# Where the split activations lie, and when each step of a pair's preparation is issued, in a hybrid attention and SwiGLU block

## The chip, the cores and the metric

The kernel runs on one core of a Trainium2 chip. The metric is device time in microseconds (us) of one execution; lower is better. TensorE (PE in the profile) multiplies; VectorE (DVE), ScalarE (ACT) and GpSimd (POOL) prepare operands; SyncE (SP) issues most loads, POOL the accumulating ones. Every engine works its own queue in order, and engines wait for each other by semaphores.

## The reference, cut to what matters

```python
xn = rms_norm(x, norm1_g)                    # x: 256 tokens x 2048
proj = xn @ w_in                             # 2048 x 5120: q, k, v, conv columns
att, u = diff_attention(...), conv_branch(...)
h = x + concat([att, u]) @ w_out             # 2048 x 2048
hn = rms_norm(h, norm2_g)
a, bu = hn @ w_gate, hn @ w_up               # 2048 x 5632 each
y = h + (silu(a) * bu) @ w_down              # 5632 x 2048
```

All of it is float32. The five weight matrices, about 200 MB, are read once.

## The kernel before, in words

**Split products.** A float32 product is made of three fast ones. Each operand is split in `hi` (rounded to the format fp32r) and `lo` (the rest, rounded too), and PE adds hi x hi, lo x hi and hi x lo in one PSUM bank. The activations are the stationary operand (128x128), loaded once per matmul; the weights are the moving one (128x512). The split activations of the input projection, of `w_out` in part, of the normalized `h` and later of the gated rows lie in two long tiles `lhi` and `llo`, the `arena`. Other activations lie in tiles of their own (`chi`/`clo`, `ahi`/`alo`, `fhi`/`flo`, `mchi`, `mahi`).

**Chunks.** All weights are cut in chunks, and `run_chunks` walks through them: at chunk t it issues what chunks ahead of t need, and then the matmuls of t. A plain chunk or "two" (`multiply_two`, 12 matmuls) holds two 128x512 weight tiles: loaded to `raw` (four buffers), cast by ACT to `whi` (L328), subtracted by DVE to `wlo` (L337). For a chunk marked `by_dma`, ACT writes -raw to `wlo` (L331) and a POOL DMA adds the weights a second time (L332), so that DVE has nothing to do.

**Pairs.** From the second gate/up block on, half of the contraction goes by a scheme of seven products in place of eight (`multiply_pair`, 21 matmuls): two contraction tiles times two sets of 512 columns make four weight tiles (`wb`, 1 MB, two buffers). Their preparation has these steps: the load; `wt`, four sum forms of the tiles, by DVE (L964 to L966, one buffer); `wh`, the casts of seven forms by ACT (L967, L968; two buffers); and the lo parts by DVE: `wla` (L978, L979; two buffers) and `wlb` (L988, L989; one buffer). `wlb` is the last reader of `wb`, so the load of the next pair but one waits for it, and all loads behind it in SP's queue wait too. The list `PRODUCTS` gives the order of the seven: PSUM bank, activation form, weight form.

**Blocks.** A gate/up block (512 columns of gate and of up; ten of them by this scheme, j = 1 to 10) has four pairs `s` and eight twos `g`, `u`; upper case marks `by_dma`. A down block has four pairs and eight twos (in the last group three and six); there are six, two behind each group of gate/up blocks (j to 3, j to 7, j to 10). `ORDER`, `FIRST` and `DOWN` give the order of the chunks. After the last pair, `bank_sums` drains its PSUM banks: ACT copies bank Q1 (L1104), DVE adds the other five into SBUF tiles (L1106 to L1112); in a gate/up block ACT then applies silu (L1118). The next block's first pair needs these banks. After the last two, `block_done` adds the last two banks, and `transposed` turns the block's result into stationary operands for the down product, at L860: by plain hi/lo (L865, L867) or, for the positions in `pairs` of `DOWN`, as seven forms (`pair_forms`, L877 to L892). This work is spread over the next block by generators that go on at each `resume()`.

**Leads.** For chunks of the scheme, loads are issued 5 chunks ahead, `by_dma` rounds 5, other rounds 3 (`round_pair`: the sums, then both casts), `wla` and `wlo` 2, `wlb` 1. `round_pair` also issues the `wlb` of the pair before it, if that is still to come.

Of the kernel before, what the change touches and what calls it, by code (L numbers as in the profile page):

```python
# [30 lines left out]
KD = D // P  # L31
N = 512
# [20 lines left out]
XPARTS = (range(0, 2), range(2, 4), range(4, 8), range(8, 12), range(12, 16))  # L53
# [3 lines left out]
AHEAD = 2  # L57
# [27 lines left out]
DOWN = (dict(pairs=((0, 0), (0, 1), (1, 0), (1, 1)), order="sgGsgGsUusUu"),  # L85
        dict(pairs=((4, 0), (4, 1), (5, 0), (5, 1)), order="sgGsgGsUusUu"),
        dict(pairs=((8, 0), (8, 1), (9, 0)), order="sgGsGsUuU"))

LOAD_AHEAD, DMA_AHEAD, HI_AHEAD, LO_AHEAD, REST_AHEAD = 5, 5, 3, 2, 1

TO_TRANSPOSE = 5

# [12 lines left out]
def tile_block(  # L105
# [179 lines left out]
    chunks = []  # L285
# [106 lines left out]
        if c["done"]:  # L392
            start(c["done"](ps))

    def run_chunks():
        n = len(chunks)
        loaded = split = rest = 0
        rounded = [0, 0]

        def load(i):  # L400
            if i in before:
                before[i]()
            chunks[i]["load"](chunks[i])

        def do_round(which, until):
            while rounded[which] < min(n, until):
                c = chunks[rounded[which]]
                if c["by_dma"] == bool(which):
                    c["round"](c)
                rounded[which] += 1  # L410

        for t in range(n):
            load_lead, dma_lead, hi_lead, lo_lead = lead(t)
            while split < min(rounded[0], t + 1 + lo_lead):
                chunks[split]["split"](chunks[split])
                split += 1
            while loaded < min(n, t + 1 + load_lead):
                load(loaded)
                loaded += 1
                if load_lead == lo_lead:  # L420
                    do_round(1, loaded)
                    do_round(0, loaded)
                    chunks[split]["split"](chunks[split])
                    split += 1
            do_round(1, t + 1 + dma_lead)
            do_round(0, t + 1 + hi_lead)
            while split < min(n, t + 1 + lo_lead):
                chunks[split]["split"](chunks[split])
                split += 1
            while rest < min(n, t + 1 + REST_AHEAD):  # L430
                split_rest(chunks[rest])
                rest += 1
# [379 lines left out]
    ffn = {}  # L812
# [23 lines left out]
    def place(g):  # L836

        pairs = DOWN[g]["pairs"]
        at = 7 * len(pairs)
# [111 lines left out]
        src = weights([(w, k, col, N) for w, col in c["sides"] for k in c["ks"]])  # L951
        sp.dma_start(out=c["b"].rearrange("p k n -> p (k n)"), in_=src)

    def round_pair(c):

        fp = ffn["pool"]
        assert "hi" in forms
        if newest:
            split_rest(newest.pop())
        newest.append(c)  # L960
        b = c["b"]
        c["t"] = t = fp.tile([P, 4, N], F32, tag="wt", name="wt")
        c["hi"] = fp.tile([P, 7, N], F32R, tag="wh", name="wh", bufs=2)
        dve.tensor_tensor(t[:, 2:4], b[:, 1:3], b[:, 0:1].to_broadcast([P, 2, N]), ALU.subtract)  # L964
        dve.tensor_tensor(t[:, 1], b[:, 1], t[:, 3], ALU.add)  # L965
        dve.tensor_tensor(t[:, 0], t[:, 1], b[:, 3], ALU.subtract)  # L966
        act.copy(c["hi"][:, 4:], b[:, 1:])  # L967
        act.copy(c["hi"][:, :4], t)  # L968

    newest = []  # L970

    def split_pair(c):

        if "lo" in c:
            return
        b, t, hi = c["b"], c["t"], c["hi"].bitcast(F32)
        lo = ffn["pool"].tile([P, 4, N], F32R, tag="wla", name="wla", bufs=2)
        dve.tensor_tensor(lo[:, 0], b[:, 2], hi[:, 5], ALU.subtract)  # L978
        dve.tensor_tensor(lo[:, 1:], t[:, 1:], hi[:, 1:4], ALU.subtract)  # L979
        c["lo"] = {5: lo[:, 0], 1: lo[:, 1], 2: lo[:, 2], 3: lo[:, 3]}  # L980

    def split_rest(c):
        if "sides" not in c or 0 in c.get("lo", ()):
            return
        split_pair(c)
        b, t, hi = c["b"], c["t"], c["hi"].bitcast(F32)
        lo = ffn["pool"].tile([P, 3, N], F32R, tag="wlb", name="wlb")
        dve.tensor_tensor(lo[:, 1], t[:, 0], hi[:, 0], ALU.subtract)  # L988
        dve.tensor_tensor(lo[:, ::2], b[:, 1::2], hi[:, 4::2], ALU.subtract)  # L989
        c["lo"].update({4: lo[:, 0], 0: lo[:, 1], 6: lo[:, 2]})  # L990

    def sum_bank(c, i):
        sums = c["sums"]
# [5 lines left out]
    def multiply_pair(c):  # L999
        while not c["ready"](c):  # L1000
            resume()
        (fhi, flo), p = c["forms"](), c["p"]
        for n, (q, f, w) in enumerate(PRODUCTS):
            ps = sum_bank(c, q)
            first, last = c["first"].get(q), c["last"].get(q)
            pe.matmul(ps, fhi[:, f, p, :], c["hi"][:, w], start=bool(first), stop=False)  # L1006
# [45 lines left out]
    def fast_block(order, side_u, side_g, pairs, twos, **kw):  # L1052
# [3 lines left out]
        for unit in order:  # L1056
# [43 lines left out]
    def bank_sums(q):  # L1100

        fp = ffn["pool"]
        w1, u2, u3, w4 = (fp.tile([P, N], F32, tag=f"sum{i}", name=f"sum{i}") for i in range(4))
        act.copy(w1, q[Q1])  # L1104
        yield
        dve.tensor_tensor(u2, q[Q6], w1, ALU.add)  # L1106
        dve.tensor_tensor(u3, q[Q7], u2, ALU.add)
        yield
        dve.tensor_tensor(w4, q[Q5], u3, ALU.add)
        dve.tensor_tensor(u2, q[Q5], u2, ALU.add)  # L1110
        dve.tensor_tensor(w1, q[Q2], w1, ALU.add)
        dve.tensor_tensor(u3, q[Q4], u3, ALU.add)  # L1112
        halfway.update(g=(w1, u3), u=(u2, w4))

    def products_done(q):
        yield from bank_sums(q)
        for t in halfway["g"]:
            act.activation(t, t, AF.Silu)  # L1118

    def block_done(j, q):  # L1120
        while "g" not in halfway:
# [9 lines left out]
    def add_to_out(m, n, t):  # L1131
        pool.dma_start(out=out[m * P : (m + 1) * P, n * N : (n + 1) * N], in_=t, accum_op=ALU.add)

    def down_products(n, q, last):
        so_far = None
        if last:
            so_far = ffn["pool"].tile([P, 4, N], F32, tag="wt", name="so_far")[:, :NM]
            pool.dma_start(out=so_far, in_=out[:, n * N : (n + 1) * N].rearrange("(m p) n -> p m n", p=P))
        yield from bank_sums(q)
        for m in range(NM):  # L1140
            add_to_out(m, n + 1, halfway["g"][m])
        if last:
            yield
# [46 lines left out]
    for g, nb in enumerate(FGROUPS):  # L1190
        for j in range(j0, j0 + nb):
            if j:
                gate_up_block(j, FIRST if j == 1 else ORDER)
                continue
# [3 lines left out]
        for n in range(0, D // N, 2):  # L1198
            down_block(g, n)
        j0 += nb  # L1200

    lead = lambda t: ((1,) * 4 if t < len(XPARTS) else (LOAD_AHEAD, DMA_AHEAD, HI_AHEAD, LO_AHEAD)
                      if "kind" in chunks[t] else (AHEAD,) * 4)
# [39 lines left out]
```

## Time and profile before

| | |
|---|---|
| median of 3 runs (lowest to highest) | 1159.44 us (1158.42 to 1162.35) |
| profiled execution: its time, its span | 1157.78 us, 1156.0 us |
| mean granted TensorE clock | 0.973 |
| busy: PE, DVE, ACT, POOL | 1080.6, 912.5, 674.0, 132.9 us |
| bytes by DMA | 247.58 MB, mean 214 GB/s |

The profile is one execution. A group row gives busy time and mean duration of an instruction, then the engine's idle time before it and what ended it. In the windows view each row is a stretch of time with the busy time of every engine in it, the granted clock (1.00 is full speed) and the DMA engines' share. In the timeline each row has the start, the length and, in brackets, the idle time before it.

### The profile page before, as it was taken

To read this page: it belongs to the slowest core of one execution; us is meant where nothing else is said; L and a number is where in the kernel's file an instruction comes from. 1 tells how busy PE (TensorE), PEld (TensorE's weight loads), DVE (VectorE), ACT (ScalarE), POOL (GpSimd) and SP (SyncE) were. 2 spreads that over 40 slices of the span, in tenths; PEclk is the share of its full clock that TensorE was granted. 3 is DMA by queue.
4 is the path that set the end of the run, shared out by engine and by line. 5 is a ranking of instruction groups with operands and counts; after the bars stand their busy time and mean duration, and the time that the engine had idled before them with its cause. 6 is when DMAs were issued, how large, how long until landed. Compare 5 with 4: busy or idle time off the path is not lost. (4 is left out here: it accounts for less than half of the span.)

```text
span 1156.0 us, 13323 instructions
## 1 busy us (share of the span) xinstructions
PE 1080.6 (93%) x4768; PEld 869.8 (75%) x4768; DVE 912.5 (79%) x1252; ACT 674.0 (58%) x857; POOL 132.9 (11%) x180
## 2 busy tenths in 40 slices
PE   8999999999999978999899998897999998999598
PEld 7888888887888856777688776676877776777486
DVE  4799889898665877887886868788788786887865
ACT  7544657656665554766556547466565454755552
POOL 1110112211001000101020201001001020101021
PEclk9999999999999989999899999999999999999899
DMA  8555544445466557779678986776968897778767
GB/s 294 193 191 189 182 164 152 170 153 180 148 203 206 203 173 245 195 248 274 199 242 250 235 274 200 254 200 206 287 205 247 246 249 244 217 247 253 212 154 182
DMA packets 62447, 247.58 MB, mean 214 GB/s; under 512 B 6964, under 2 KB 8430, under 8 KB 54444
## 3 DMA queue, kind: packets, MB, share of 16 engines
q1 hardware_dynamic: 48000, 200.56, 48.0%
q0 software_dynamic: 14320, 46.14, 21.3%
q8 instruction: 37, 0.61, 0.2%
q14 instruction: 30, 0.25, 0.1%
q10 hardware_dynamic: 60, 0.03, 0.0%
HBM read 238.31 MB, written 8.39 MB: 213 GB/s over the span
## 5 line engine op out<-in xcount | busy, mean ns | idle before, releaser
L328 ACT CAST whi<-raw 128x1024 fp32r<-128x1024 f32 (+1 forms) x253 | 260.2, 1045 | 167.8 <-DMA raw<-in_wts_dram 125.6
L337 DVE TENSOR_TENSOR wlo<-raw,whi 128x1024 fp32r<-128x1024 f32 (+1 forms) x181 | 219.0, 1217 | 57.0 <-ACT whi L328 56.6
L968 ACT CAST wh<-wt 128x2048 fp32r<-128x2048 f32 x62 | 118.3, 1908 | 101.9 <-DVE wt L966 101.9
L367 PE MATMUL acc<-whi,lhi 128*128 128x512 f32 (+1 forms) x448 | 170.8, 386 | 3.3 <-ACT lhi L234 2.6
L368 PE MATMUL acc<-whi,llo 128*128 128x512 f32 (+1 forms) x448 | 169.1, 382 | 0.5 <-DVE llo L235 0.4
L979 DVE TENSOR_TENSOR wla<-wt,wh 128x1536 fp32r<-128x1536 f32 x62 | 108.9, 1757 | 64.3 <-ACT wh L968 64.3
L1006 PE MATMUL q<-wh,fhi 128*128 128x512 f32 x280 | 118.1, 422 | 31.8 <-DVE sum L1110 18.0
L332 POOL DMA_DIRECT2D wlo<-in_wts_dram x72 | 67.6, 939 | 634.2 <-ACT wlo L331 500.1
L1024 PE MATMUL q<-whi,chi 128*128 128x512 f32 x320 | 124.8, 390 | 0.0
L1025 PE MATMUL q<-whi,clo 128*128 128x512 f32 x320 | 124.6, 389 | 0.0
L373 PE MATMUL acc<-wlo,lhi 128*128 128x512 f32 (+1 forms) x448 | 116.4, 384 | 0.0
L1007 PE MATMUL q<-wh,flo 128*128 128x512 f32 x280 | 114.5, 409 | 0.0
L524 DVE SCALAR_TENSOR_TENSOR y<-upad,cw,y 128x256 f32<-128x256 f32 x240 | 103.7, 482 | 4.6 <-ACT y L517 4.1
L367 PEld LDWEIGHTS acc<-whi,lhi 128*128 128x128 f32 x448 | 85.3, 190 | 20.7 <-ACT lhi L234 2.8
L368 PEld LDWEIGHTS acc<-whi,llo 128*128 128x128 f32 x448 | 85.4, 191 | 17.7 <-DVE llo L235 0.9
L1006 PEld LDWEIGHTS q<-wh,fhi 128*128 128x128 f32 x280 | 56.0, 200 | 50.1 <-DVE sum L1110 21.4
L373 PEld LDWEIGHTS acc<-wlo,lhi 128*128 128x128 f32 x448 | 79.9, 189 | 16.9 <-DVE wlo L337 0.2
L967 ACT CAST wh<-wb 128x1536 fp32r<-128x1536 f32 x62 | 90.8, 1465 | 2.9 <-PE q L1007 1.5
L1029 PE MATMUL q<-wlo,chi 128*128 128x512 f32 x320 | 86.5, 392 | 0.0
L964 DVE TENSOR_TENSOR wt<-wb 128x1024 f32<-128x1024 f32 x62 | 75.5, 1218 | 3.8 <-DMA wb<-in_wts_dram 3.8
L331 ACT ACTIVATE wlo<-raw 128x1024 fp32r<-128x1024 f32 x72 | 76.0, 1055 | 0.0
L989 DVE TENSOR_TENSOR wlb<-wb,wh 128x1024 fp32r<-128x1024 f32 x62 | 75.5, 1218 | 0.0
(219 smaller groups left out, 1870.9 us busy)
## 6 DMA issues: line engine op xcount, KB each, us to landing
raw<-in_wts_dram SPq DMA_DIRECT2D x251, 512.0 KB, 5.5
wb<-in_wts_dram SPq DMA_DIRECT2D x62, 1024.0 KB, 5.3
wlo<-in_wts_dram POOLq DMA_DIRECT2D x72, 512.0 KB, 8.0
out_dram<-sum POOLq DMA_DIRECT2D x22, 256.0 KB, 8.8
out_dram<-h POOLq DMA_DIRECT2D x8, 256.0 KB, 5.2
h<-in_x_dram SPq DMA_DIRECT2D x6, 256.0 KB, 7.8
h<-in_x_dram SPq DMA_DIRECT2D x4, 128.0 KB, 2.9
raw<-in_wts_dram SPq DMA_DIRECT2D x2, 256.0 KB, 3.9
```

What stands on the lines that cost most here:

```text
L328: act.copy(c["hi"], c["raw"])
L337: dve.tensor_tensor(c["lo"], c["raw"], c["hi"].bitcast(F32), ALU.subtract)
L367: pe.matmul(ps[m], xhi[:, ms], hi[:, j, :], start=c["first"] and j == 0, stop=False)
L368: pe.matmul(ps[m], xlo[:, ms], hi[:, j, :], start=False, stop=False)
L373: pe.matmul(ps[m], xhi[:, ms], lo[:, j, :], start=False, stop=c["last"] and j == nk - 1)
L524: dve.scalar_tensor_tensor(y[:, ct, :], src, wk, y[:, ct, :], ALU.mult, ALU.add)
L968: act.copy(c["hi"][:, :4], t)
L979: dve.tensor_tensor(lo[:, 1:], t[:, 1:], hi[:, 1:4], ALU.subtract)
L1006: pe.matmul(ps, fhi[:, f, p, :], c["hi"][:, w], start=bool(first), stop=False)
L1007: pe.matmul(ps, flo[:, f, p, :], c["hi"][:, w], start=False, stop=False)
L1024: pe.matmul(ps, plain[i][0][:, ms], hi[:, i, :], start=i == 0 and bool(c["first"].get(qs[m])), stop=False)
L1025: pe.matmul(ps, plain[i][1][:, ms], hi[:, i, :], start=False, stop=False)
```

## The change

1. The arena is allocated right after `ident`, ahead of small tiles. Its two tiles start at byte 128 of a 512-byte line of each partition, as nearly all other tiles do; before, at byte 480. Sizes are unchanged.
2. `round_pair` is parted: `pair_sums` (the DVE sums) gets a lead of its own, 4 chunks; the casts stay at 3, `wla` at 2, `wlb` at 1. Loads are issued last in a step, not first.
3. `wla` is now the four sum forms in one instruction of 2048 elements, `wlb` the three raw forms in one of 1536 (before: 512 + 1536, and 512 + 1024).
4. `PRODUCTS` starts with the three sum forms; bank Q1, which was first, is fourth. So `wlb` is first needed by the 12th of a pair's 21 matmuls.
5. `ORDER` and the down orders have the pairs at chunks 0, 2, 5, 7 of 12 and four twos at the end (before: 0, 3, 6, 9 and two). `FIRST` has them at 3, 5, 7, 9 (before 4, 6, 8, 10). Down blocks have three `by_dma` chunks (the last two blocks too) where they had four; `FIRST` four where it had three.
6. `bank_sums` is issued in one piece, not over three `resume()`s. In the first group the down pairs come from j = 1 and 2, not 0 and 1.

```diff
-ORDER = "sgGsgGsUUsUu"
+ORDER = "sGsGgsGsUuUu"
-FIRST = "gugusgsUsGsU"
+FIRST = "gugsGsGsusUU"
-PRODUCTS = ((Q1, 0, 5), (Q6, 5, 1), (Q7, 6, 2), (Q5, 4, 3), (Q2, 1, 6), (Q4, 2, 0), (Q3, 3, 4))
-DOWN = (dict(pairs=((0, 0), (0, 1), (1, 0), (1, 1)), order="sgGsgGsUusUu"),
+PRODUCTS = ((Q6, 5, 1), (Q7, 6, 2), (Q5, 4, 3), (Q1, 0, 5), (Q2, 1, 6), (Q4, 2, 0), (Q3, 3, 4))
+DOWN = (dict(pairs=((1, 0), (1, 1), (2, 0), (2, 1)), order="sGsGgsGsuuuu"),
...
-        dict(pairs=((8, 0), (8, 1), (9, 0)), order="sgGsGsUuU"))
-LOAD_AHEAD, DMA_AHEAD, HI_AHEAD, LO_AHEAD, REST_AHEAD = 5, 5, 3, 2, 1
+        dict(pairs=((8, 0), (8, 1), (9, 0)), order="sGsGgsUuu"))
+LOAD_AHEAD, DMA_AHEAD, SUMS_AHEAD, HI_AHEAD, PART_AHEAD, REST_AHEAD = 5, 5, 4, 3, 2, 1
...
     make_identity(nc, ident)
+    arena = [const.tile([P, 2 * KD, P], F32R, tag=f"l{x}", name=f"l{x}") for x in ("hi", "lo")]
...
-    arena = [const.tile([P, 2 * KD, P], F32R, tag=f"l{x}", name=f"l{x}") for x in ("hi", "lo")]
...
         for t in range(n):
...
+            if "kind" in chunks[t]:
+                until("part", part_of, t + 1 + PART_AHEAD)
+                until("dma", round_of, t + 1 + DMA_AHEAD, lambda c: c["by_dma"])
+                until("sums", sums_of, t + 1 + SUMS_AHEAD)
+                until("round", round_of, t + 1 + HI_AHEAD)
+                until("rest", rest_of, t + 1 + REST_AHEAD)
+                load_until(t + 1 + LOAD_AHEAD)
+            else:
+                until("rest", rest_of, t + 1 + (1 if t < len(XPARTS) else AHEAD))
+            rest_of(t)
             chunks[t]["multiply"](chunks[t])
...
-    def round_pair(c):
+    def pair_sums(c):
...
         if newest:
-            split_rest(newest.pop())
+            part_of(newest.pop())
...
-        act.copy(c["hi"][:, 4:], b[:, 1:])
-        act.copy(c["hi"][:, :4], t)
...
+    def round_pair(c):
+        c["hi"] = ffn["pool"].tile([P, 7, N], F32R, tag="wh", name="wh", bufs=2)
+        act.copy(c["hi"][:, 4:], c["b"][:, 1:])
+        act.copy(c["hi"][:, :4], c["t"])
+
     def split_pair(c):
...
+        c["lo"] = ffn["pool"].tile([P, 4, N], F32R, tag="wla", name="wla", bufs=2)
+        dve.tensor_tensor(c["lo"], c["t"], c["hi"][:, :4].bitcast(F32), ALU.subtract)
 
     def split_rest(c):
...
+        c["lob"] = ffn["pool"].tile([P, 3, N], F32R, tag="wlb", name="wlb")
+        dve.tensor_tensor(c["lob"], c["b"][:, 1:], c["hi"][:, 4:].bitcast(F32), ALU.subtract)
...
-            pe.matmul(ps, fhi[:, f, p, :], c["lo"][w], start=False, stop=bool(last))
+            pe.matmul(ps, fhi[:, f, p, :], c["lo"][:, w] if w < 4 else c["lob"][:, w - 4], start=False, stop=bool(last))
...
         act.copy(w1, q[Q1])
-        yield
         dve.tensor_tensor(u2, q[Q6], w1, ALU.add)
         dve.tensor_tensor(u3, q[Q7], u2, ALU.add)
-        yield
...
```

VectorE's queue where block j = 5 ends and j = 6 begins, before (`wb`, `wt`, `wh`, `wla`, `wlb` as above; `sum` are the drained banks, `q` the banks):

```order
L966 TENSOR_TENSOR wt<-wt,wb 128x512
L978 TENSOR_TENSOR wla<-wb,wh 128x512
L979 TENSOR_TENSOR wla<-wt,wh 128x1536
L1106 TENSOR_TENSOR sum_6210<-q_5913,sum_6209 128x512
L1107 TENSOR_TENSOR sum_6211<-q_5917,sum_6210 128x512
L337 TENSOR_TENSOR wlo<-raw,whi 128x1024
L988 TENSOR_TENSOR wlb<-wt,wh 128x512
L989 TENSOR_TENSOR wlb<-wb,wh 128x2x512
L1109 TENSOR_TENSOR sum_6212<-q_5921,sum_6211 128x512
L1110 TENSOR_TENSOR sum_6210<-q_5921,sum_6210 128x512
L1111 TENSOR_TENSOR sum_6209<-q_5925,sum_6209 128x512
L1112 TENSOR_TENSOR sum_6211<-q_5929,sum_6211 128x512
```

and now:

```order
L1115 TENSOR_TENSOR sum_6117<-q_5864,sum_6116 128x512
L1116 TENSOR_TENSOR sum_6115<-q_5864,sum_6115 128x512
L1117 TENSOR_TENSOR sum_6114<-q_5872,sum_6114 128x512
L1118 TENSOR_TENSOR sum_6116<-q_5876,sum_6116 128x512
L337 TENSOR_TENSOR wlo<-raw,whi 128x1024
L994 TENSOR_TENSOR wla<-wt,wh 128x2048
L981 TENSOR_TENSOR wt<-wb 128x1024
L982 TENSOR_TENSOR wt<-wb,wt 128x512
L983 TENSOR_TENSOR wt<-wt,wb 128x512
L998 TENSOR_TENSOR wlb<-wb,wh 128x1536
L1132 TENSOR_TENSOR sum_6115<-q_5880,sum_6115 128x512
```

Before, the first pair's `wt` and `wla` stand ahead of the bank sums, and its `wlb` between them. Now the sums come first in one piece (the last four are shown), then the first pair's `wla`, the `wt` of the second pair, and the first pair's `wlb` behind that.

ScalarE's queue at the same place, before:

```order
L967 CAST wh<-wb 128x1536
L968 CAST wh<-wt 128x2048
L328 CAST whi<-raw 128x1024
L1104 COPY sum_6209<-q_5909 128x512
L1118 ACTIVATE sum_6209<-sum_6209 128x512
L1118 ACTIVATE sum_6211<-sum_6211 128x512
L328 CAST whi<-raw 128x1024
L331 ACTIVATE wlo<-raw 128x1024
```

and now:

```order
L1112 COPY sum_6114<-q_5868 128x512
L1124 ACTIVATE sum_6114<-sum_6114 128x512
L1124 ACTIVATE sum_6116<-sum_6116 128x512
L989 CAST wh<-wb 128x1536
L990 CAST wh<-wt 128x2048
L328 CAST whi<-raw 128x1024
L331 ACTIVATE wlo<-raw 128x1024
L989 CAST wh<-wb 128x1536
L990 CAST wh<-wt 128x2048
```

Before, both casts of the next block's first pair stand ahead of the copy of bank Q1 and of the silu. Now they come behind the silu, which waits for the bank sums; behind them is a `by_dma` two and then the casts of the second pair.

More of the change, by code (lines that the diff above doesn't have):

```diff
@@ L393, in multiply, with load_until @@
             start(c["done"](ps))
[L395 to L400, printed above, removed]
+    loaded, rounded, parted, whole = [0], set(), set(), set()
+    def load_until(n):
+        while loaded[0] < min(n, len(chunks)):
+            i = loaded[0]
+            loaded[0] += 1
             if i in before:
@@ L403, in load, with sums_of @@
             chunks[i]["load"](chunks[i])
[L405 to L410, printed above, removed]
-        for t in range(n):
[L413 to L432, printed above, removed]
+    def sums_of(i):
+        c = chunks[i]
+        if "sides" in c and "t" not in c:
+            load_until(i + 1)
+            pair_sums(c)
@@ new lines, in round_of, with part_of, rest_of, run_chunks @@
+    def round_of(i):
+        if i not in rounded:
+            rounded.add(i)
+            load_until(i + 1)
+            sums_of(i)
+            chunks[i]["round"](chunks[i])
+    def part_of(i):
+        if i not in parted:
+            parted.add(i)
+            round_of(i)
+            chunks[i]["split"](chunks[i])
+    def rest_of(i):
+        if i not in whole:
+            whole.add(i)
+            part_of(i)
+            if "sides" in chunks[i]:
+                split_rest(chunks[i])
+    def run_chunks():
+        n = len(chunks)
+        at = dict(part=0, dma=0, sums=0, round=0, rest=0)
+        def until(what, do, stop, only=lambda c: True):
+            while at[what] < min(n, stop):
+                if only(chunks[at[what]]):
+                    do(at[what])
+                at[what] += 1
+        for t in range(n):
+            if "kind" in chunks[t]:
[8 more added lines that the diff above has]
+            rest_of(t)
@@ L952, in load_pair @@
         sp.dma_start(out=c["b"].rearrange("p k n -> p (k n)"), in_=src)
[L954 to L956 removed]
+    def pair_sums(c):
         assert "hi" in forms
         if newest:
[L959 to L960 removed]
+            part_of(newest.pop())
+        newest.append(next(i for i, o in enumerate(chunks) if o is c))
         b = c["b"]
[L962 to L963 removed]
+        c["t"] = t = ffn["pool"].tile([P, 4, N], F32, tag="wt", name="wt")
         dve.tensor_tensor(t[:, 2:4], b[:, 1:3], b[:, 0:1].to_broadcast([P, 2, N]), ALU.subtract)
```

26 lines of the change are left out of this document (5 added, 21 removed).

## The prediction

> **What bounds the kernel now.** First the windows view by stage, then the waits, then rows of single steps.
>
> ```profile
> core 0: us, PE busy (x) PEld busy (x) DVE busy (x) ACT busy (x) POOL busy (x), PEclk, DMA share, GB/s
> 0.00:401.88 401.88, 396.12 (x1890) 326.45 (x1891) 320.67 (x526) 240.34 (x449) 50.19 (x85) 1.00 0.53 186
> 401.88:455.48 53.60, 44.53 (x190) 35.99 (x188) 40.32 (x53) 31.38 (x31) 3.55 (x4) 0.90 0.69 226
> 455.48:1072.94 617.46, 572.37 (x2412) 454.80 (x2412) 492.69 (x602) 366.23 (x346) 67.01 (x77) 0.97 0.80 235
> 1072.94:1152.20 79.26, 67.53 (x278) 52.53 (x278) 58.04 (x72) 36.05 (x33) 12.14 (x14) 0.94 0.71 187
> ```
>
> Up to 401.88 (projections, attention, `w_out`, the plain block) PE is the bound. Then run the pair blocks: the first (to 455.48), thirteen more, and the last two down blocks (from 1072.94). There PE idles 9.1 + 45.1 + 11.7 = 65.9 us, and a stretch at half clock loses half its length, so the clock's shortfall costs 10%, 3% and 6% of the three stretches: 5.4 + 18.5 + 4.8 = 28.7 us.
>
> ```profile
> PE q L1006 <- DVE sum L1110: 22.4, 11, 3.1
> DVE wla L979 <- ACT wh L968: 64.3, 50, 1.4
> SPq L952 <- DVE wlb L989: 625.3, 60, 16.2
> 509.19 0.50 PE L1006 MATMUL q<-wh,fhi 128*128 128x512 f32 x1 [2.18 <-DVE sum L1110]
> ...
> 510.97 0.63 PE L1006 MATMUL q<-wh,fhi 128*128 128x512 f32 x1
> 643.86:691.79 47.93, 43.70 (x182) 34.66 (x180) 35.86 (x41) 26.14 (x22) 7.91 (x9) 0.96 0.91 260
> 739.89:789.16 49.27, 45.07 (x188) 35.20 (x189) 40.15 (x56) 30.74 (x32) 4.33 (x5) 0.97 0.75 221
> 789.16:840.82 51.66, 45.57 (x190) 36.40 (x189) 43.13 (x52) 28.26 (x26) 4.33 (x5) 0.93 0.75 219
> ```
>
> A block's first pair waits for the bank sums; a pair's preparation goes DVE, ACT, DVE, and DVE waits for ACT in the middle; every pair load waits for a `wlb`. Behind a gap of 2.18 us, matmuls take 0.63 us in place of 0.39: half clock. The last three rows are gate/up blocks (j = 4, 6, 7).
>
> **The arena.** Three starts on, with `lhi`/`llo` and then with `chi`/`clo`; medians in the source view; weight loads:
>
> ```profile
> 382.88 0.40 PE L368 MATMUL acc<-whi,llo 128*128 128x512 f32 x1
> ...
> 383.59 0.40 PE L367 MATMUL acc<-whi,lhi 128*128 128x512 f32 x1
> ...
> 402.81 0.39 PE L1024 MATMUL q<-whi,chi 128*128 128x512 f32 x1
> ...
> 403.49 0.39 PE L1025 MATMUL q<-whi,clo 128*128 128x512 f32 x1
> ...
> L367 PE MATMUL acc<-whi,lhi 128*128 128x512 f32 x384 | 153.7, 400 | 0.0
> L373 PE MATMUL acc<-wlo,lhi x448: 277/394/585, 8.3 to 401.6; 128*128 128x512 f32 x128, 128*128 128x256 f32 x22
> L1029 PE MATMUL q<-wlo,chi x320: 388/389/481, 403.7 to 1071.4; 128*128 128x512 f32 x160
> L367 PEld LDWEIGHTS acc<-whi,lhi 128*128 128x128 f32 x448 | 85.3, 190 | 20.7 <-ACT lhi L234 2.8 <-ACT whi L328 1.0
> L1024 PEld LDWEIGHTS q<-whi,chi 128*128 128x128 f32 x320 | 60.3, 188 | 12.9
> ```
>
> A matmul costs 0.71 / 3 = 0.237 us with the arena and 0.68 / 3 = 0.227 without, 10 ns apart; the medians (394, 389) lie 5 apart. The arena is the one stationary tile that starts at byte 480. I take 7 ns. Three lines of 384 such matmuls (one is shown) stand in the first stretch, where PE is never late: 1152 x 0.007 = 8.1 us, by the two ends 5.8 to 11.5. The pair blocks are reckoned below at 0.227 throughout. DVE has 401.88 - 320.67 = 81 us to spare there, so nothing is late next. The Trainium skill says in "TensorE: Matmul & The Clock Gate", LDWEIGHTS, that a weight load's time follows its column count alone; the two load rows agree (190, 188), and by that rule the start byte buys nothing and the sum is 8.1 us higher. The starts differ nonetheless, with the same `whi` buffers, so I go by them.
>
> **The steps.** Durations, in order of the path: bank sums, sums of a pair, `wla`, a subtraction of 2048 elements, the seven-form work of a block's result, then ACT's silu and casts, then loads of a pair and of `raw`:
>
> ```profile
> 744.99 0.68 DVE L1110 TENSOR_TENSOR sum<-q,sum 128x512 f32<-128x512 f32 x1
> 745.59 0.68 DVE L1111 TENSOR_TENSOR sum<-q,sum 128x512 f32<-128x512 f32 x1
> ...
> 749.18 1.22 DVE L964 TENSOR_TENSOR wt<-wb 128x1024 f32<-128x1024 f32 x1
> ...
> 751.16 0.69 DVE L966 TENSOR_TENSOR wt<-wt,wb 128x512 f32<-128x512 f32 x1
> ...
> 753.83 1.76 DVE L979 TENSOR_TENSOR wla<-wt,wh 128x1536 fp32r<-128x1536 f32 x1 [1.38 <-ACT wh L968]
> 755.51 0.29 DVE L883 SCALAR_TENSOR_TENSOR fs<-af 128x128 f32<-128x128 f32 x1
> ...
> 756.44 1.22 DVE L337 TENSOR_TENSOR wlo<-raw,whi 128x1024 fp32r<-128x1024 f32 x1
> ...
> 759.32 0.42 DVE L889 TENSOR_TENSOR llo<-af,lhi 128x256 fp32r<-128x256 f32 x1
> ...
> L946 DVE TENSOR_TENSOR flo<-sums,fhi x1: 2285/2285/2285, 391.7 to 391.7; 128x2048 fp32r<-128x2048 f32 x1
> 746.30 1.29 ACT L1118 ACTIVATE sum<-sum 128x512 f32<-128x512 f32 x2 [6.47 <-DVE sum L1111]
> 749.39 1.47 ACT L967 CAST wh<-wb 128x1536 fp32r<-128x1536 f32 x1
> 751.89 1.91 ACT L968 CAST wh<-wt 128x2048 fp32r<-128x2048 f32 x1 [1.03 <-DVE wt L966]
> 757.08 1.05 ACT L328 CAST whi<-raw 128x1024 fp32r<-128x1024 f32 x1
> DMA to landing us min/median/max: 4.6/5.3/10.1
> raw<-in_wts_dram SPq DMA_DIRECT2D x251, 512.0 KB, 5.5
> ```
>
> Starts follow 0.08 us before the end of the instruction ahead, so I take 0.6 for a bank sum, 2.6 for a pair's sums, 2.2 for the new `wla`, 1.7 for the new `wlb` (the old 1.76, same size), 1.1 for `wlo`, 0.9 and 1.1 for the two halves of the seven-form work, 3.2 for both casts `wh`. A pair is 21 x 0.227 = 4.76 us of PE, a two 2.72. The merged subtractions are two instructions in place of four: 2.2 + 1.7 against 0.6 + 1.7 + 0.6 + 1.1, 0.1 saved per pair, which is in the run below. `by_dma` falls by one chunk in each of six down blocks and rises by one in the first pair block: five more `wlo` of 1.1 on DVE, late in blocks where it is not awaited (the run for down blocks keeps 1 us of margin there), five casts and five accumulating loads fewer on ACT and POOL: nothing either way. SP issues the same loads in chunk order as before; POOL's output adds stand, as before, between a block's last `by_dma` loads and the next block's, whose weights are wanted 17 us later: nothing.
>
> A gate/up block that follows another and does its seven-form work, counted from x, the end of its predecessor's last pair (s0, s2, s5, s7 are its own, by chunk number). PE has four twos, 10.9. ACT copies Q1 by x + 0.7, DVE adds until 4.6, silu ends 5.3, and only then come the casts of s0: 8.5. DVE idles from 5.7 (`wlo`) to 8.5; `wla` 10.7; sums of s2 13.3; `wlb` of s0 15.0. PE starts s0 at 10.9 and wants it with the 12th matmul, 13.4: **1.6 us late**; s0 ends 17.3. The load of s5 goes at 15.0, lands 20.4; DVE does the block sums and `wla` of s2 till 19.6, waits, sums of s5 23.0, `wlb` of s2 24.7, wanted 22.9: **1.8 late**. ACT stands at the `by_dma` cast of chunk 6 till its `raw` lands behind that load, 21.5; two casts, one for chunk 4, the copy of the transposed result 25.1; DVE's seven-form work, `wlo` 28.3; casts of s5 29.8, `wla` 32.0, sums of s7 34.6, more seven-form work, `wlb` of s5 37.7, wanted 35.3: **2.4 late**. s5 ends 39.9, s7 47.4. So a block takes 47.4; j = 6 took 49.3. The wait for the bank sums is gone (they end 6 us before the pair starts); what is late next is `wlb`, in the queue behind the next pair's sums.
>
> The same run without silu and seven-form work (behind a down block) has `wlb` of s0 at 12.2, in time, one wait of 1.0 and 41.9 in all; j = 4 took 47.9. With plain transposes: 45.2; j = 7 took 51.7. Half clock cost the thirteen blocks 18.5 us, 1.4 each; PE running late inside a block is absorbed by the next `wlb` wait, whose end DVE sets, so only the last wait's spell counts. I add the old 1.4 to the first kind, 0.4 and 0.9 to the others, by their number of waits. The same page of the Trainium skill, under "Why this matters for your kernels", asks only that gaps stay under about 3 us; the trace has half clock behind 2.18. By that rule these 12.7 us would not come, 1110. Of the thirteen blocks, six are of the first kind (48.8), four of the second (42.3), three of the third (46.1): 600.3 against 617.5, **-17.2**.
>
> **The ends.** The last two down blocks are 6 pairs and 12 twos, 61.2, with transposes 0.7. Before, they waited, beside the first pair's bank sums, for the block's own result:
>
> ```profile
> PE q L1024 <- ACT lhi L865: 4.2, 1, 4.2
> PE q L1025 <- DVE llo L867: 3.6, 1, 3.6
> ```
>
> That two is now one pair later (4.8 us) and its lo ready. With 1.6 + 1.8 of `wlb` waits, 1.0 clock and 0.9 at the last pairs: 67.2, **-12.1**. The first pair block: the first pair comes a chunk earlier, but its banks still wait for both transposes, the second now behind a third pair's sums, whose load waits for the first `wlb`: about 3 later, and one two more behind it; two chunks in place of one before the next block's first pair give most of it back: +1, between -5 and +6.
>
> **The sum.** -8.1 - 17.2 - 12.1 + 1 = -36.4. The profiled execution took 1157.78, so 1121.4; the median of the runs is 1.7 higher: 1123.
>
> **The rivals.**
> - *PE-bound.* If the steps' leads hide everything, thirteen blocks take some 42 each (4 x 4.76 + 8 x 2.72 = 40.8, transposes 0.7), 546: 54 us better than my run, 1069. For it, a down block that ran without a gap:
>
> ```profile
> 602.16:643.86 41.70, 41.70 (x181) 33.84 (x180) 30.95 (x35) 21.84 (x18) 7.05 (x8) 1.00 0.89 257
> ```
>
> Against: with silu and seven-form work DVE needs 40 (40.15 in the row of j = 6) of 42 us and waits for ACT on top. Chance of ending under 1090: 0.13.
> - *The chain of loads, slower than before.* One pair load is in flight at a time: `wlb` frees the buffer, the load lands, DVE (in order) does its sums and only then the next `wlb`. Each microsecond of landing over 5.3 is paid once per block, 13 times. The gain of 36 is gone at 2.8 more, a landing of 8.1; at the row's maximum, 10.1, it is 62 us: 1185. For it: DMA at 0.91 of its share in the fast block. Against: the median of 5.3 holds at shares of 0.8. Chance: 0.08.
> - *The arena changes nothing.* Nearly all `chi` matmuls stand in other stages than those with `lhi`; if the 7 ns belong to the stage and not to the address, 8.1 us stay: 1131. Against: quiet PE in both stretches of the rows. Chance 0.06. The rule on weight loads above would come out here.
> - *The waits only move.* If every block loses to the clock what j = 7 lost, 0.07 x 51.66 = 3.6 us, in place of 1.4, 0.4 and 0.9, that is +34: 1157, no change. For it: my run's first kind of block still has three waits of about 2 us. Chance 0.09.
>
> My case holds 0.64. Under 0.3% (3.5 us) a measurement of this kernel tells nothing from no change. Of the fourth rival most falls there; with the tail of my case: faster 0.84, same 0.07, slower 0.09. Range: my run is uncertain by 2 us a block, 26 in all, and the arena by 3; downward it takes in part of the PE-bound rival: 1088 to 1150.
>
> **What would show it.** Matmuls with `lhi` at 389 ns; PE's waits for the bank sums nearly gone, those for `wlb` the longest; blocks behind down blocks near 42 us, the first kind near 48; no wait for `lhi` in the last down blocks. Wrong if pair loads land in over 8 us, or if `wlb` comes in time everywhere.

## The result: 3.5% slower, where 3% faster was forecast

| | before | after |
|---|---|---|
| median (lowest to highest) | 1158.93 us (1156.94 to 1162.35) | 1197.55 us (1195.11 to 1207.27) |
| profiled execution, its span | 1157.78, 1156.0 us | 1195.49, 1193.7 us |
| mean granted clock | 0.973 | 0.962 |

The ratio is 1.0346, 95% interval 1.0281 to 1.0410; 1123 was forecast, in a range of 1088 to 1150. Here and below, all times and rows are of executions with a mean granted clock of 0.95 to 0.99; one of the four executions of run 4, the profiled one, ran at 0.65 and is left out.

The stages of the changed kernel, in the windows view with the columns as before:

```profile
0.00:397.78 397.78, 389.92 (x1890) 325.62 (x1891) 320.09 (x526) 240.25 (x449) 52.58 (x85) 1.00 0.57 188
397.78:463.74 65.96, 49.46 (x190) 38.04 (x188) 39.02 (x35) 30.49 (x27) 4.57 (x6) 0.84 0.62 187
463.74:1113.90 650.16, 578.28 (x2413) 459.02 (x2413) 495.79 (x516) 364.34 (x348) 63.44 (x73) 0.96 0.75 221
1113.90:1189.94 76.04, 68.55 (x278) 53.85 (x278) 57.90 (x57) 33.56 (x30) 10.44 (x12) 0.93 0.69 180
```

The first stretch is 4.1 us shorter, the first pair block 12.4 longer, the thirteen blocks 32.7 longer, and the last two 3.2 shorter: +37.7. PE idles 71.9 us in the thirteen blocks, 45.1 before. The waits of PE, DVE and ACT, each with total, times and longest:

```profile
PE q L1016 <- DVE wlb L998: 62.7, 37, 4.2
PE q L1016 <- DVE wla L994: 14.3, 9, 1.6
PE q L1014 <- ACT wh L990: 5.2, 9, 0.6
...
DVE sum L1113 <- ACT sum L1112: 58.2, 16, 5.9
...
ACT whi L328 <- DMA raw<-in_wts_dram: 203.5, 43, 10.1
```

PE's waits for bank sums have gone, as forecast, and the waits for `wlb` are the longest. The fourth row is new. DVE stands at its first bank sum until ACT has copied bank Q1. Of the kernel before, the same view has

```profile
DVE sum L1106 <- ACT sum L1104: 2.5, 1, 2.5
```

The timeline shows how this wait and those for `wlb` hang together. This is where a block's last pair ends, at 555.3, and the next block's first pair begins: ACT, then DVE, then PE.

```profile
552.52 1.05 ACT L328 CAST whi<-raw 128x1024 fp32r<-128x1024 f32 x1 [4.44 <-DMA raw<-in_wts_dram]
...
557.18 1.05 ACT L328 CAST whi<-raw 128x1024 fp32r<-128x1024 f32 x1 [2.65 <-issue]
558.14 0.58 ACT L1112 COPY sum<-q 128x512 f32<-128x512 f32 x1
562.26 1.29 ACT L1124 ACTIVATE sum<-sum 128x512 f32<-128x512 f32 x2 [3.54 <-DVE sum L1117]
...
558.75 0.69 DVE L1113 TENSOR_TENSOR sum<-q,sum 128x512 f32<-128x512 f32 x1 [5.12 <-ACT sum L1112]
...
566.76 2.29 DVE L994 TENSOR_TENSOR wla<-wt,wh 128x2048 fp32r<-128x2048 f32 x1 [2.80 <-ACT wh L990]
569.09 1.23 DVE L981 TENSOR_TENSOR wt<-wb 128x1024 f32<-128x1024 f32 x1
...
571.69 1.75 DVE L998 TENSOR_TENSOR wlb<-wb,wh 128x1536 fp32r<-128x1536 f32 x1
...
556.72 0.39 PE L1033 MATMUL q<-whi,clo 128*128 128x512 f32 x1
...
566.78 0.50 PE L1014 MATMUL q<-wh,lhi 128*128 128x512 f32 x1 [0.61 <-ACT wh L990]
...
569.11 0.50 PE L1016 MATMUL q<-wla,lhi 128*128 128x512 f32 x1 [1.60 <-DVE wla L994]
...
573.49 0.50 PE L1016 MATMUL q<-wlb,lhi 128*128 128x512 f32 x1 [2.04 <-DVE wlb L998]
...
575.47 0.63 PE L1016 MATMUL q<-wla,lhi 128*128 128x512 f32 x1
```

In ACT's queue the copy stands behind a cast of a `raw` chunk that begins only at 557.18. That cast does not wait for a load. It writes a `whi` buffer, of which there are four, and it begins 0.07 us after the end of PE's eighth matmul of the two behind the pair (556.72 + 0.39), the last of that two to read `whi`: it waits for PE to free a buffer. The view names nothing as the end of this idle time ("issue"), but at other blocks' ends it names PE, as here:

```profile
607.77 1.05 ACT L328 CAST whi<-raw 128x1024 fp32r<-128x1024 f32 x1 [3.14 <-PE q L1033]
```

In every one of the thirteen blocks the cast ahead of the copy begins 1.85 to 1.90 us after the end of the last pair's matmuls and within 0.1 us of the end of that eighth matmul, and no load is named as what ended its wait. In the kernel before, the cast ahead of the copy did not wait in any of them. So the copy comes 2.85 us after the pair's end, the bank sums end 7.5 after it and the silu 8.3. The casts, the `wla` and the `wlb` of the first pair follow: PE waits for all three, 4.25 us in one pair, and from 574.6 the rest of the pair runs at half clock. The `wlb` stands behind the next pair's sums (569.09 to 571.8).

Two faults can be read from this, and the experiments try both. **Copy:** ACT's copy of Q1 comes late, behind a cast that waits for PE, and everything on DVE comes late with it. **Row:** `wlb` is queued behind the next pair's sums. Rivals: the uneven spacing of the pairs (one two between them), the longer landing of pair loads (median 6.8 us, 5.3 before), the product order, the early sums, the first block's string.

### The profile page after: what moved, and what is told of

Same layout as the page of the kernel before. It is cut to its first block, busy times and chain, and to the rows that moved or that the text cites. A ratio compares the mean times of both kernels' runs of the same rounds, so it can differ in the third digit from the quotient of the medians.

```text
span 1193.7 us, 13200 instructions
## 1 busy us (share of the span) xinstructions
PE 1086.2 (91%) x4768; PEld 876.5 (73%) x4768; DVE 913.6 (77%) x1133; ACT 668.6 (56%) x852; POOL 131.0 (11%) x175
## 4 chain that ended last, share of the span: by engine, by line
PE 22%; DVE 18%; DMA 13%; ACT 12%; issue 4%; SPq 0%; DVEq 0%; ACTq 0%
DMA raw<-in_wts_dram 8%; DMA wb<-in_wts_dram 5%; ACT wh L990 5%; PE q L1016 4%; DVE wla L994 4%; PE q L1032 4%; PE q L1033 4%; PE q L1014 3%; PE q L1015 3%; PE q L1037 3%; DVE wt L981 3%; ACT wh L989 2%; DVE wlb L998 2%; ACT whi L328 2%; DVE wt L982 2%
## 5 line engine op out<-in xcount | busy, mean ns | idle before, releaser
L328 ACT CAST whi<-raw 128x1024 fp32r<-128x1024 f32 (+1 forms) x253 | 259.9, 1046 | 277.4 <-DMA raw<-in_wts_dram 203.5
L337 DVE TENSOR_TENSOR wlo<-raw,whi 128x1024 fp32r<-128x1024 f32 (+1 forms) x186 | 224.5, 1217 | 51.7 <-ACT whi L328 50.6
L994 DVE TENSOR_TENSOR wla<-wt,wh 128x2048 fp32r<-128x2048 f32 x62 | 141.9, 2289 | 72.9 <-ACT wh L990 72.9
L332 POOL DMA_DIRECT2D wlo<-in_wts_dram x67 | 59.2, 884 | 664.3 <-ACT wlo L331 664.3
L1032 PE MATMUL q<-whi,chi 128*128 128x512 f32 x320 | 128.4, 401 | 0.0
L1033 PE MATMUL q<-whi,clo 128*128 128x512 f32 x320 | 127.1, 397 | 0.0
L998 DVE TENSOR_TENSOR wlb<-wb,wh 128x1536 fp32r<-128x1536 f32 x62 | 108.6, 1751 | 5.9 <-PE q L1016 5.9
L1016 PE MATMUL q<-wlb,fhi 128*128 128x512 f32 x120 | 54.4, 453 | 44.3 <-DVE wlb L998 44.3
```

The lines of the kernel that those rows point to most:

```text
L328: act.copy(c["hi"], c["raw"])
L337: dve.tensor_tensor(c["lo"], c["raw"], c["hi"].bitcast(F32), ALU.subtract)
L994: dve.tensor_tensor(c["lo"], c["t"], c["hi"][:, :4].bitcast(F32), ALU.subtract)
L998: dve.tensor_tensor(c["lob"], c["b"][:, 1:], c["hi"][:, 4:].bitcast(F32), ALU.subtract)
L1032: pe.matmul(ps, plain[i][0][:, ms], hi[:, i, :], start=i == 0 and bool(c["first"].get(qs[m])), stop=False)
L1033: pe.matmul(ps, plain[i][1][:, ms], hi[:, i, :], start=False, stop=False)
```

## Experiments

All are compared with the kernel before; times are medians. Where `wlb` is issued earlier, the lines of the pair code are one or two higher (L1016 is L1018).

**1. The arena alone.**

```diff
     make_identity(nc, ident)      # in the kernel before
+    arena = [const.tile([P, 2 * KD, P], F32R, tag=f"l{x}", name=f"l{x}") for x in ("hi", "lo")]
```

> The kernel before with the arena's tile lists moved to the start, nothing else. Theory A (the start byte costs each of 1152 512-column matmuls 7 ns): starts of matmuls with lhi/llo go from 234 to 227 ns and the time falls by 4 (what the same stage gave in the changed kernel, 401.9 to 397.8) to 8 us, 1151 to 1155. Theory B (the address does nothing, the changed kernel's first stage was shorter by its new order of steps): spacing stays 234, time within 2 us of before.

1153.2 us, ratio 0.9954 (0.9935 to 0.9972): -5.7 by the medians of that comparison. Groups by form, of the kernel before and then of this one; the third group stands in the prediction for before (153.7):

```profile
L368 PE MATMUL acc<-whi,llo 128*128 128x512 f32 x384 | 152.1, 396 | 0.0
L373 PE MATMUL acc<-wlo,lhi 128*128 128x512 f32 x384 | 106.9, 400 | 0.0
```

```profile
L367 PE MATMUL acc<-whi,lhi 128*128 128x512 f32 x384 | 151.5, 395 | 0.0
L368 PE MATMUL acc<-whi,llo 128*128 128x512 f32 x384 | 149.8, 390 | 0.0
L373 PE MATMUL acc<-wlo,lhi 128*128 128x512 f32 x384 | 104.8, 395 | 1.8 <-DVE wlo L337 1.8
```

2.2 + 2.3 + 2.1 = 6.6 us of busy time gone, 5.7 ns a matmul, and 1.8 of it spent on a new wait for `wlo`. The median distance of two starts goes from 234 to 227 ns, as theory A said, and theory A holds. The Trainium skill, "TensorE: Matmul & The Clock Gate", LDWEIGHTS, gives a weight load's time by its column count alone. The weight loads agree with it (190 ns before and here); what changed is the distance of the matmuls, so it does not follow from that rule that the edit is worth nothing.

**2. The row.** `wlb` of the pair ahead is issued ahead of the next pair's sums wherever its one buffer allows.

```diff
...
-            part_of(newest.pop())
+            (rest_of if len(newest) < 2 or now[0] > newest[-2] else part_of)(newest[-1])
```

> The changed kernel, but the wlb of the pair ahead is issued on DVE ahead of the next pair's sums wherever its single buffer allows (as the kernel before did), in place of behind them. Theory A (queue): waits of L1016 for wlb, 62.7 us in 37 times, fall under 20 us, and the time to 1150 to 1165. Theory B (spacing): waits fall by less than a third, 1180 to 1195. Theory C (bank sums in one piece): 1185 to 1197.

1163.8 us, ratio 1.0039 (1.0021 to 1.0057): 34 us back, theory A. In the changed kernel's trace 47 of 62 `wlb` stand behind the next pair's sums, in this one 2, before none. Waits of this kernel:

```profile
PE q L1018 <- DVE wla L996: 25.9, 21, 1.6
PE q L1016 <- ACT wh L992: 14.2, 14, 1.7
...
PE q L1018 <- DVE wlb L1000: 2.1, 3, 1.1
...
DVE sum L1115 <- ACT sum L1114: 42.1, 14, 4.9
...
ACT whi L328 <- DMA raw<-in_wts_dram: 109.5, 33, 6.7
```

The wait for `wlb` is gone, and part of it comes back at `wla` and `wh`, the steps before it. A `wlb` that comes sooner also frees its `wb` sooner, and the loads behind it follow: ACT's wait for `raw` is 109.5 us, 203.5 in the changed kernel. The pair loads land as late as in the changed kernel (median 6.8), so their landing is not what made it slower.

**3. The old strings in the changed kernel.**

```diff
-ORDER = "sGsGgsGsUuUu"     # FIRST and DOWN likewise
+ORDER = "sgGsgGsUUsUu"
```

> The changed kernel with the old strings ORDER, FIRST and DOWN (pairs at chunks 0, 3, 6 and 9, two chunks between, in place of 0, 2, 5, 7); split steps, merged subtractions, product order and arena stay new. Theory A (queue: wlb stands in DVE's row behind the next pair's sums, which wait for a load that the wlb before released; spacing matters little): 1185 to 1197. Theory B (spacing: with one two between pairs PE wants the next wlb 7.5 us after the last one, less than the chain of load, sums, cast and subtractions takes): most of 38 us comes back, 1150 to 1165. Theory C (bank sums in one piece hold DVE): 1190 to 1197.

1219.0 us, ratio 1.0514 (1.0488 to 1.0540): slower still, outside all three ranges. That the new spacing made the changed kernel slow falls: without it the time grows, here and in run 8, where `wlb` is in time. With pairs three chunks apart in most blocks, the next sums come ahead of `wlb` nearly every time: 60 of 62 in its trace. DVE hardly waits for ACT's copy any more, though the bank sums are in one piece.

```profile
PE q L1016 <- DVE wlb L998: 103.4, 40, 5.9
...
DVE sum L1113 <- ACT sum L1112: 5.4, 2, 2.8
```

**4. Bank sums in three parts again.**

```diff
         act.copy(w1, q[Q1])
+        yield
         dve.tensor_tensor(u2, q[Q6], w1, ALU.add)
         dve.tensor_tensor(u3, q[Q7], u2, ALU.add)
+        yield
...
```

> The changed kernel, with the bank sums handed out in three parts between the steps again, as in the kernel before (silu and the output adds behind them as before). Theory C (DVE stands 58.2 us at the first bank sum for ACT's copy of Q1, and what is queued behind it is late): 1165 to 1180. Theories A and B: DVE's wait there shrinks, but PE then waits for the bank sums again (22 us before), 1190 to 1205.

1174.0 us, ratio 1.0139 (1.0112 to 1.0166): 24 back (the expectations below reckon with 22), as theory C has it.

**5. The copy by DVE.**

```diff
-        act.copy(w1, q[Q1])
+        dve.tensor_copy(w1, q[Q1])
```

> The changed kernel, with the copy of bank Q1 made by DVE in place of ACT, bank sums still in one piece: DVE's 58.2 us of waiting for ACT's copy are gone, 16 copies of 0.7 us (11 us) are added to DVE. Theory C (the wait for ACT's copy is what the one-piece bank sums cost): as much back as with the bank sums in parts, 1172 to 1182. Rival (the parts helped since other work of DVE's came between them): 1190 to 1200.

1154.3 us, ratio 0.9963 (0.9943 to 0.9984): 43 back, more than either theory gave, though DVE does 11 us more. The same place as above, ACT and then DVE (the last pair ends at 554.7 here), its waits, and the thirteen blocks:

```profile
556.56 1.05 ACT L328 CAST whi<-raw 128x1024 fp32r<-128x1024 f32 x1 [3.43 <-issue]
557.51 1.15 ACT L1124 ACTIVATE sum<-sum 128x512 f32<-128x512 f32 x2
...
553.39 0.69 DVE L1113 TENSOR_TENSOR sum<-q,sum 128x512 f32<-128x512 f32 x1
...
556.64 0.68 DVE L1118 TENSOR_TENSOR sum<-q,sum 128x512 f32<-128x512 f32 x1
```

```profile
PE q L1016 <- DVE wlb L998: 59.5, 39, 4.3
...
PE q L1016 <- DVE wla L994: 1.7, 4, 0.9
...
464.60:1076.69 612.09, 562.27 (x2413) 450.79 (x2413) 506.80 (x529) 359.23 (x337) 63.34 (x73) 0.98 0.80 235
```

The bank sums run while the pair still multiplies and end 2.7 us after it, though the cast of ACT is as late as before (1.9 us after the pair). PE's waits for `wh` and `wla` go; those for `wlb` stay nearly as they were. Of the 38.1 us that the thirteen blocks gain, 22.1 are idle time of PE (49.8 for 71.9) and 16.0 are busy time for the same matmuls (562.3 for 578.3), at a granted clock of 0.98 for 0.96.

**6. Both undone:** 2 and 4 together.

> The changed kernel with both undone: wlb issued ahead of the next pair's sums, and the bank sums in three parts. Theory A (two separate faults on DVE: wlb alone gave 34 us, the bank sums alone 22): they add to some 50, 1140 to 1150, faster than before. Theory B (one fault seen twice: each edit only takes DVE's stand at the head of the same row away): the second edit adds under 8 us to the first, 1156 to 1166.

1140.6 us, ratio 0.9849 (0.9823 to 0.9875). 34 and 24 would add to 58, and 57 came: theory A.

**7. The new strings in the kernel before.**

> The kernel before with the new strings ORDER, FIRST and DOWN (pairs at 0, 2, 5, 7), nothing else. Theory A (the new order of units is good by itself: a last pair two chunks earlier leaves four twos for the bank sums, whose waits of 26 us go; the loss comes from the steps): 1135 to 1152. Theory B (with one two between pairs, preparation, which keeps the old steps, comes too late): 1165 to 1190.

1187.2 us, ratio 1.0252 (1.0221 to 1.0282). Theory B's range; but its waits show more than late preparation:

```profile
PE q L1008 <- DVE wla L979: 22.4, 30, 1.1
...
DVE sum L1106 <- ACT sum L1104: 71.6, 15, 7.9
```

With the new strings the old kernel too has DVE standing at ACT's copy (2.5 us before), though its bank sums are in parts; with the old strings the changed kernel has not (5.4 us in run 3), though they are in one piece. So the copy's wait comes with the strings, which put the last pair two chunks earlier: four twos now stand behind it, and the cast that waits until PE has read the first of them gets ahead of the copy. Here too it begins 1.9 us after the last pair.

**8. Both undone, with the old strings.**

> As the run with both undone, and with the old strings ORDER, FIRST and DOWN too: left of the change are the arena, the merged subtractions, the product order and the earlier sums (4 chunks ahead). Theory A (the new order is worth something once wlb is in time): 8 to 25 us slower than the run with both undone, since PE waits for the bank sums again. Theory B (the order is worth nothing): within 5 us of it. Arena and merged subtractions alone would put it at 1148 to 1154.

1172.9 us, ratio 1.0136 (1.0107 to 1.0164): 32 slower than 6. With the steps in time the new strings are worth more than expected; PE waits 43.2 us for the bank sums without them. That it is 15 slower than the kernel before was expected by neither theory, and why stays open.

**9. Row and copy together,** 2 and 5.

> The changed kernel with wlb issued ahead of the next pair's sums and bank Q1 copied by DVE; the bank sums stay in one piece. Theory A (two separate faults: the copy that stands on ACT behind a cast that waits for its load, 43 us; wlb in the row behind sums that wait for their load, 34 us): they add, 1115 to 1130. Theory B (both act through the lateness of the same wlb): 1138 to 1150, no better than the run with both undone (1140.6).

1129.9 us, ratio 0.9762 (0.9736 to 0.9787). At the upper end of theory A's range: of 34 + 43 = 77, 68 came. (The cast ahead of the copy waits for PE, not for its load, as shown above.)

**10. Row, copy and parts,** 2, 4 and 5: with runs 14 and 15 the fastest kernel.

> As the run with both undone (wlb ahead of the sums, bank sums in three parts), and bank Q1 copied by DVE besides. Theory A (the parts helped only by letting other work in while ACT's copy was awaited): no better than wlb first with DVE's copy in one piece, within 6 us of it. Theory B (parts are worth something by themselves): 8 us or more faster than that run.

1117.3 us, ratio 0.9649 (0.9625 to 0.9672). 12.7 faster than 9, so theory B: the parts are worth something even with no copy to wait for. Stages and waits:

```profile
398.00:461.67 63.67, 45.91 (x191) 35.99 (x191) 41.59 (x37) 32.34 (x28) 5.26 (x6) 0.91 0.70 208
461.67:1046.19 584.52, 554.33 (x2412) 448.59 (x2413) 501.84 (x530) 357.65 (x336) 63.29 (x73) 0.99 0.83 245
1046.19:1112.00 65.81, 63.92 (x279) 52.39 (x277) 54.65 (x57) 30.02 (x26) 9.66 (x12) 0.97 0.76 208
...
PE q L1018 <- DVE wla L996: 18.7, 16, 1.6
PE q L1016 <- DVE alo L887: 6.0, 1, 6.0
PE q L1016 <- ACT wh L992: 6.0, 4, 1.7
PE q L1016 <- DVE sum L1114: 6.0, 1, 6.0
```

**11. The copy by DVE in the kernel before,** with the arena.

> The kernel before with the arena's tiles moved and bank Q1 copied by DVE in place of ACT; its bank sums stay in three parts. Theory A (the late copy costs only where the bank sums are in one piece and end in the pair's own queue; before, DVE waited 2.5 us for it in all): 1148 to 1158, as the arena alone (1153.2). Theory B (the copy behind ACT's cast was the wait of PE for the bank sums before too, 26 us): 1125 to 1142.

1163.9 us, ratio 1.0049 (1.0032 to 1.0066): 11 slower than the arena alone, 6 over theory A's range and far from theory B's. Where ACT reaches the copy in time, moving it does not help: PE's waits for the bank sums go from 29.0 us with the arena alone to 45.0.

**12. Both undone, with the old product order.**

> As the run with both undone, and with the old order of products (Q1, which reads a wlb form, first; in the new split its low part is wanted with the third matmul in place of the twelfth, 2 us earlier). Theory A (wlb is in time there, PE waited for it 1.1 us in all): within 5 us of 1140.6. Theory B (the order of products is what hides wlb): 15 to 60 us slower.

1158.6 us, ratio 1.0004 (0.9986 to 1.0022), 18 slower than 6: theory B, at its lower end.

```profile
PE q L1018 <- DVE wlb L1000: 65.4, 50, 3.6
```

`wlb`, wanted at a pair's third matmul, is late 50 times; in 6 it was so twice, 1.6 us in all.

**13 to 15. The first pair block.** The old `FIRST` in the changed kernel; the same in kernel 10; and there with the old pairs of the first group too.

> The changed kernel with the old string FIRST alone (first pair at chunk 4 in place of 3, and two chunks apart as before). Theory A (the pair that stands a chunk earlier waits for the transposes of the block before and for their low halves, 10.1 us): 5 to 12 us back, 1184 to 1192. Theory B (the wait is for the transposes, wherever the pair stands, since DVE comes to their subtractions late): within 3 us of the changed kernel, 1194 to 1200.

> The fastest so far (wlb ahead of the sums, bank sums in parts, Q1 copied by DVE; 1117.3) with the old string FIRST. Theory A: 5 to 12 us faster, 1105 to 1112. Theory B: within 3 us, 1114 to 1120.

> As the run before with the old string FIRST, and with the old pairs of the first group's down blocks too ((0,0), (0,1), (1,0), (1,1) in place of (1,0) to (2,1)): the block 0 result gets its seven forms in the first pair block, block 2's does not. Theory A (plain transposes in place of seven forms free DVE where it is latest): 3 to 10 us slower than the run with the old string alone. Theory B (the pairs move the same work from one block to another): within 3 us of it.

1189.9 us, ratio 1.0284 (1.0225 to 1.0344); 1115.9 us, 0.9617 (0.9587 to 0.9648); 1116.8 us, 0.9624 (0.9594 to 0.9655). The first interval overlaps that of the changed kernel, so that run is unclear; the other two lie within 1.4 us of run 10, theory B each time. With the old string in kernel 10 the first pair hardly waits for `llo` and `alo` any more (0.5 us for 9.7), and the first pair block ends 4.7 us earlier; but the thirteen blocks behind it take 588.9 us in place of 584.5, so next to nothing is left.

**16. Sums 3 chunks ahead,** in kernel 10.

```diff
-LOAD_AHEAD, DMA_AHEAD, SUMS_AHEAD, HI_AHEAD, PART_AHEAD, REST_AHEAD = 5, 5, 4, 3, 2, 1
+LOAD_AHEAD, DMA_AHEAD, SUMS_AHEAD, HI_AHEAD, PART_AHEAD, REST_AHEAD = 5, 5, 3, 3, 2, 1
```

> The fastest so far (1117.3) with a pair's sums 3 chunks ahead in place of 4, so at the same place as its casts. Theory A (the earlier sums are worth something once nothing else holds DVE: casts of ACT find them ready): 8 to 25 us slower, 1125 to 1142. Theory B (the early sums cost: they reach DVE ahead of their load): 3 to 10 us faster, 1107 to 1114.

1178.8 us, ratio 1.0163 (1.0135 to 1.0191): 62 slower than 10, far more than theory A's 25. In this kernel the sums carry the `wlb` of the pair ahead with them, and that `wlb` frees the buffer for a load; so the edit moves three steps, and the 62 us are not the sums' alone. How they divide stays open, and so does what the earlier sums are worth.

## Why the prediction was wrong

Of the 74 us between forecast and result of the profiled execution (1121.4 and 1195.5), 49.9 arose in the thirteen blocks, 11.4 in the first pair block, 8.9 in the last two and 4.0 in the first stretch.

**The step that failed** is one line of the hand-run: "ACT copies Q1 by x + 0.7, DVE adds until 4.6, silu ends 5.3", where x is the end of a block's last pair. It took ACT to be free at x. Measured in the block shown: 3.4, 7.5 and 8.3. ACT was not free, since the cast ahead of the copy waited until PE had read its `whi` buffer for the last time, 1.8 us after x. The hand-run did let ACT stand at a cast until its `raw` landed, later in the same block, but it had no term for a cast that waits for a buffer. The shift of 3 us runs through the rest of the hand-run unchanged: the casts of the next block's first pair end at 11.4 in place of 8.5, its `wla` at 13.8 in place of 10.7, its `wlb` at 18.1 in place of 15.0. PE loses 4.25 us in this pair, where 1.6 were forecast. Run 5 takes DVE's wait for ACT's copy away by another way, and then the hand-run's sum comes out within 2%:

| mean us of a block | hand-run | after | copy by DVE | kernel 10 |
|---|---|---|---|---|
| first kind (6) | 48.8 | 51.6 | 49.4 | 46.3 |
| behind a down block (4) | 42.3 | 48.0 | 43.9 | 44.1 |
| plain transposes (3) | 46.1 | 49.6 | 46.8 | 43.4 |
| thirteen blocks | 600.3 | 650.2 | 612.1 | 584.5 |

(From the starts of the blocks' first pairs.) So of the 50 us by which the thirteen blocks missed, 38 went with ACT's copy. The copy by DVE is a little better than the hand-run assumed (its sums end at x + 2.7, not 4.6), so 38 may be more than this step's part; what the other 12 are stays open.

**Right in kind:** "what is late next is `wlb`, in the queue behind the next pair's sums". It was (62.7 us), and run 2 shows that its place in the row did it. The forecast priced it at 1.6, 1.8 and 2.4 us in a block of the first kind and 1.0 in one behind a down block. It did not ask whether the changed kernel needed that row at all. The waits for the bank sums went, and the wait for `lhi` too, as forecast. Neither of the two signs of being wrong that it named came: pair loads land in 6.8 us, under 8, and `wlb` was late.

**The arena:** right that the place of the tiles matters; 7 ns was taken and 7 measured between starts, 5.7 in busy time, and the first stretch gave 4.1 of the 8.1 us. The rival that it changes nothing falls.

**The last two down blocks:** -12.1 forecast, -3.2 measured. In kernel 10 these blocks take 65.8 us, against the forecast's 67.2, so the same copy and row stood in the way, or the parts.

**The first pair block:** +1 forecast (-5 to +6), +12.4 measured. The term said that a delay of about 3 us and one more two would for the most part be given back by the two chunks before the next block's first pair. In the trace PE waits 3.8 us for `llo` and 6.3 for `alo` in the first pair, and 5 more for `wlb` later; of the 12.4 us, 7.4 are idle time and 4.9 busy time, at a granted clock of 0.84 for 0.90. Runs 14 and 15 move this wait without shortening the total, run 13 is unclear, and in kernel 10 the block still takes 63.7. What sets it stays open.

**The rivals.** The chain of loads was to give 1185 by long landings, breaking even at 8.1 us; the time came near it by luck: the landing was 6.8, for which that rival's own price gives 1.5 x 13 = 20 us and not 62, and runs 2, 6 and 10 won their time back with landings of 6.8, 6.9 and 6.7. "The waits only move" was nearest in kind: they moved from the bank sums to `wlb`, and grew. No run came near the PE-bound rival: the thirteen blocks take 584.5 us at best, against its 546.

**What the change's parts are worth** depends on their company. The new strings cost 29 us in the old steps (run 7 against before) and gain 32 in the new steps once `wlb` comes ahead of the sums and the bank sums are in parts (run 6 against 8). The order of products is worth 18 there. The one-piece bank sums, with ACT's copy at their head, and the late `wlb` cost 57 together (after against run 6).

## What to carry to other kernels

When work is moved to the front of an in-order queue, look at what its first instruction waits for on the other engine, and at what stands ahead of that there. Here a copy of 0.6 us stood behind a cast that could not begin before PE had freed its buffer, and everything behind the copy came late with it. A wait for a buffer is as real a wait as one for a load, and it has to be in the hand-run. Issue the step that frees a buffer, or that is wanted next, ahead of a step that must itself wait for a load. And before a regrouping is given up as slower, undo its parts one by one: three small edits turned +3.5% into -3.5%.

## What was not expected of the hardware

Where a stationary tile starts shows in matmul spacing: from byte 480 of a 512-byte line to byte 128, median starts come 227 ns apart in place of 234 and busy time falls by 5.7 ns for each of 1152 matmuls (run 1), with weight loads of the same length. That it is the place in the line, and not another side of the address, is not shown.

Half clock does not follow from one gap's length. Two pairs of the changed kernel, each with one gap:

```profile
621.18 0.50 PE L1016 MATMUL q<-wlb,lhi 128*128 128x512 f32 x1 [1.89 <-DVE wlb L998]
...
622.21 0.63 PE L1014 MATMUL q<-wh,lhi 128*128 128x512 f32 x1
...
1168.99 0.50 PE L1016 MATMUL q<-wlb,lhi 128*128 128x512 f32 x1 [2.57 <-DVE wlb L998]
...
1170.71 0.39 PE L1014 MATMUL q<-wh,lhi 128*128 128x512 f32 x1
```

A gap of 1.89 us is followed by matmuls of 0.63 us, one of 2.57 by none. The Trainium skill, "TensorE: Matmul & The Clock Gate", under "Why this matters for your kernels", asks for no idle gaps of PE over about 3 us. Keeping to that does not keep a kernel from half clock here, and since the longer of these two gaps is the harmless one, no other single length would part them.
